# Layer 0's down projections at sixteen pairs of row and weight places with three wider products each; output tiles innermost and stepped sums elsewhere

## The chip, the core and the metric

The kernel runs on one core of one Trainium2 chip. TensorE (PE) multiplies, VectorE (DVE) and ScalarE (ACT) prepare operands and take sums out of PSUM, GpSimd (POOL) does small copies, SyncE (SP) issues the transfers of the weights. The metric is the device time of one execution in microseconds; three runs of the kernel before gave 2278.22, 2278.60 and 2279.71.

## What is computed

A decoder of two layers over 272 positions (16 meta tokens and 256 inputs) with model width 2048, 16 heads of 128 and an MLP of width 8192. Layer 0 is a forgetting attention, layer 1 a stick-breaking attention over shared keys and values.

```python
for layer in range(2):
    a = rms_norm(h, norm_attn[layer])
    ...                       # attention of the layer, its output projection added to h
    h = h + squared_relu_mlp(rms_norm(h, norm_mlp[layer]), w_up[layer], w_down[layer])
return rms_norm(h, final_norm)[:, N_META:]

def squared_relu_mlp(h, w_up, w_down):
    u = h @ w_up
    return jnp.square(jax.nn.relu(u)) @ w_down
```

Everything is in float32. Only the 256 inputs are returned, so the kernel drops the 16 meta positions from layer 1's queries on.

## The kernel before

Activations lie feature-major: 16 chunks of 128 features on the partitions, positions along the free axis. Every projection is a run of `gemm_group` calls (line 174). One call makes 512 output features, four tiles `acc` of 128 features, from all 16 chunks of the input and one block of weights. To keep float32 accuracy with the single-pass type fp32r, rows and weights are each split in a high and a low part, and a product is three matmuls: weight high by row high, weight high by row low, weight low by row high. So a call issues 4 tiles x 16 chunks x 3 = 192 matmuls, each with a weight load of its own, and the 96 calls issue 18,432, all recorded at line 162 in the helper `gemm_matmul`. That helper also chains each matmul behind the one before it, so TensorE's order is the order in which the code writes them (except in the first call, where the scheduler orders them).

A call goes through its 16 chunks in four blocks `kb` of four. In blocks 0 and 3 all chunks of one output tile come before the next tile. In blocks 1 and 2 the weights come in two halves of two chunks; within a half the code before runs for `m` (output tile), for `kc` (chunk), for the three pairs of parts. Layer 1's calls (`t0` = 16) run the pairs of parts outermost. Weights arrive by SP's queue in `raw`, ACT writes the high part `whi` (line 214), DVE the low part `wlo` (line 215), each as 128 x 1024 elements; four buffers of each.

Two lengths of product occur. Calls for all positions (`t0` = 0: layer 0, the shared keys and values) stream 272 columns, calls for layer 1's inputs (`t0` = 16) stream 256.

Where operands lie is written out by hand. The class `Split` (line 99) holds the high and low rows of one activation, 640 numbers a chunk; `ROWS` says where in the chunk they begin: high at 48 and low at 368 for 272 columns, 0 and 320 for 256 columns. Weights begin at number 0 of their tile for 272 columns and at number 16 for 256. All tiles and strides are multiples of 64 numbers (256 bytes), so counted modulo 64 the rows begin 48 after the weights in both cases.

For 256 columns there is one thing more. In every second call the argument `widen` makes three of the first block's products six columns longer (262; line 234, `over`). The six columns beyond the row are zeros that POOL copied there (line 114, `SPAN` = 6), and the sums in them are not used. Calls of 272 columns have no such products.

The MLP (`mlp`) runs four slices `f` of 2048 hidden features; each slice is four up calls (from `xm`, writing the new `Split` `u`) and four down calls (from `u`, adding to `hT`).

Of the kernel before, what the change touches and what calls it, by code (L numbers as in the profile page):

```python
# [9 lines left out]
F32 = mybir.dt.float32  # L10
# [5 lines left out]
P = 128  # L16
D = 2048
NC = D // P
M = 16
# [8 lines left out]
SPAN = 6  # L28
# [6 lines left out]
def yoco_kernel(ctx: ExitStack, tc: tile.TileContext, hT_in, gains, b_f, w_f, w_qkv0, w_o0, w_up, w_dn,  # L35
# [63 lines left out]
    class Split:  # L99


        def __init__(self, label, t0):
            n = T - t0
            self.t0 = t0
            rows = xs.tile([P, NC * XROW + 64], F32R, tag="x", name=f"x_{label}")
            hi, lo = ROWS[t0]
            o = min(hi, lo)
            rows = rows[:, o:o + NC * XROW].rearrange("p (c t) -> p c t", c=NC)
            self.hi, self.lo = (rows[:, :, k - o:k - o + n] for k in (hi, lo))

            if t0:
                self.wide = {}
                for name, k in (("hi", hi), ("lo", lo)):
                    nc.gpsimd.tensor_copy(rows[:, 0, k - o + n:k - o + n + SPAN], pad[:, :SPAN])
                    self.wide[name] = rows[:, 0, k - o:k - o + n + SPAN]

    def split_chunk(sp, gi, c):

# [51 lines left out]
        tc.add_manual_dep(ins.ins, queued[0].name, mybir.DependencyInfo(mybir.DependencyClass.NoSync,  # L170
                                                                        mybir.DependencyReason.DATA))

    def gemm_group(wblk, sp, t0, evac, before={}, after={}, load_x=None, widen=False):

        uid[0] += 1
        u = uid[0]  # L180
        accs = [pacc.tile([P, 512], F32, tag="acc", name=f"acc_{u}_{m}") for m in range(4)]
        n = T - t0
        for kb in range(4):
            src_w = wblk[kb].rearrange("p (k c) -> p k c", k=4)
            if kb in before:
                before[kb]()
            piece = 1 if load_x is not None and kb < 2 else 2
            raws = [wraw.tile([P, 2, 512], F32, tag="raw", name=f"raw_{u}_{kb}_{hf}") for hf in range(2)]
            for k0 in range(0, 4, piece):
                if load_x is not None:  # L190
                    load_x(range(4 * kb + k0, 4 * kb + k0 + piece))
                if load_x is not None and kb == k0 == 0:

                    for c0 in (0, 256):
                        nc.scalar.dma_start(raws[0][:, 0, c0:c0 + 256], src_w[:, 0, c0:c0 + 256])
                else:
                    nc.sync.dma_start(raws[k0 // 2][:, k0 % 2:k0 % 2 + piece], src_w[:, k0:k0 + piece])
            parts = []
            for hf in range(2):
                whi = wspl.tile([P, 2 * 576], F32R, tag="whi", name=f"whi_{u}_{kb}_{hf}")  # L200
                wlo = wspl.tile([P, 2, 576], F32R, tag="wlo", name=f"wlo_{u}_{kb}_{hf}")
                if t0:
                    whi = whi.rearrange("p (k c) -> p k c", k=2)[:, :, 16:528]
                    wlo = wlo[:, :, 16:528]
                else:
                    whi = whi[:, :1024].rearrange("p (k c) -> p k c", k=2)
                    wlo = wlo[:, :, :512]
                boxes = [(o, piece, 0, 512) for o in range(0, 2, piece)]
                if load_x is not None and kb == hf == 0:
                    boxes[:1] = [(0, 1, 0, 256), (0, 1, 256, 512)]  # L210
                for o, no, c0, c1 in boxes:
                    src = raws[hf][:, o:o + no, c0:c1]
                    hp, lp = whi[:, o:o + no, c0:c1], wlo[:, o:o + no, c0:c1]
                    on_act = nc.scalar.activation(hp, src, AF.Copy)  # L214
                    on_dve = nc.vector.tensor_tensor(out=lp, in0=src, in1=hp.bitcast(F32), op=ALU.subtract)  # L215
                parts.append((whi, wlo))
            if kb in after:
                with tc.issue_after(on_act.ins), tc.issue_after(on_dve.ins):
                    after[kb]()


            if load_x is not None and kb == 0:
                runs = [([kc], range(4)) for kc in range(4)]
            elif kb in (0, 3):
                runs = [(range(4), [m]) for m in range(4)]
            else:
                runs = [(range(2 * hf, 2 * hf + 2), range(4)) for hf in range(2)]
            pinned[0] = load_x is None
            for kcs, ms in runs:
                if t0:  # L230
                    series = [(w, x, kc, m) for w, x in ((0, "hi"), (0, "lo"), (1, "hi")) for m in ms for kc in kcs]
                else:
                    series = [(w, x, kc, m) for m in ms for kc in kcs for w, x in ((0, "hi"), (0, "lo"), (1, "hi"))]
                for i, (w, x, kc, m) in enumerate(series):
                    over = SPAN if widen and kb == m == 0 and i in (0, 4, 8) else 0
                    rhs = sp.wide[x] if over else getattr(sp, x)[:, 4 * kb + kc]
                    gemm_matmul(accs[m][:, :n + over], parts[kc // 2][w][:, kc % 2, m * P:(m + 1) * P], rhs,
                                start=kb == kc == w == 0 and x == "hi", stop=kb == kc == 3 and w == 1)
                if kb == 3:
                    for m in ms:  # L240
                        evac(m, accs[m][:, :n])
# [297 lines left out]
    def mlp(layer, xm, norm, t0, last_evac):  # L539
# [3 lines left out]
            box["r"] = norm.finish()  # L543

        for f in range(N_FF):
            u = Split(f"u{layer}_{f}", t0)
            for g in range(4):
                def evac(m, acc, g=g):
                    c = 4 * g + m
                    r = tmp.tile([P, T], F32, tag="relu", name=f"relu_{layer}_{f}_{c}")  # L550
                    u2 = tmp.tile([P, T], F32, tag="u2", name=f"u2_{layer}_{f}_{c}")
                    nc.vector.scalar_tensor_tensor(out=r[:, t0:], in0=acc, scalar=0.0, in1=box["r"][:, t0:],
                                                   op0=ALU.max, op1=ALU.mult)
                    nc.scalar.activation(u2[:, t0:], r[:, t0:], AF.Square)
                    nc.scalar.activation(u.hi[:, c], u2[:, t0:], AF.Copy)
                    nc.vector.tensor_tensor(out=u.lo[:, c], in0=u2[:, t0:], in1=u.hi[:, c].bitcast(F32),
                                            op=ALU.subtract)
                gemm_group(w_up[layer, f, g], xm, t0, evac, {2: get_rstd} if f == g == 0 else {},
                           widen=t0 == M and g % 2 == 1)
            for g in range(4):  # L560
                def evac(m, acc, g=g):
                    residual_add(4 * g + m, acc, t0)
                    if f == N_FF - 1:
                        last_evac(4 * g + m)
                gemm_group(w_dn[layer, f, g], u, t0, evac, widen=t0 == M and g % 2 == 1)

    xm, norm_m = out_proj(w_o0, ao, 0, G_M0, "m0", late, turning)

# [182 lines left out]
```

## Time and profile before

| | |
|---|---|
| median of three runs | 2278.60 us |
| the profiled execution | 2278.99 us |
| its span, first to last instruction | 2277.3 us |
| mean granted TensorE clock | 0.998 |
| TensorE busy in the span | 2265.0 us |
| VectorE, ScalarE busy | 1360.6 us, 1111.8 us |
| layer 0's MLP, 32 calls | 418.4 to 1176.6 us from the span's start |
| of it the first slice's four down calls | 513.6 to 608.3 us |
| shared keys and values, 8 calls | 1264.7 to 1473.9 us |

A matmul's record reads about 280 ns because its end is modelled with the pipeline's depth, and records overlap. What a matmul costs is the distance from its start to the next start. It is read by dividing a window by the number of matmuls in it, or from two rows of the timeline (start, length, count): the difference of the starts by the count of the first row.

### The profile page before, as it was taken

The page shows a single profiled execution, that of the slowest core. Times are in us where ns is not written, and L with a number is a line of the kernel's source. Part 1 is how long each engine was busy: PE and PEld are TensorE (multiplying, and loading weights), DVE is VectorE, ACT ScalarE, POOL GpSimd, SP SyncE. Part 2 cuts the span into 40 slices and gives each one's busy share as a digit, 9 for nine tenths or more (in the row PEclk, how much of TensorE's full clock was granted, in tenths as well). Part 3 has the DMA queues.
Part 4 walks back from the last instruction along what each step waited for, and adds up shares of the span by engine and source line. Part 5 has one row for each costly group of instructions (what it writes and reads, how often), then busy time and mean ns, then how long its engine had stood idle before and what let it go on. Part 6 is the DMA issues. An engine that isn't in the chain of part 4 may idle for free.

```text
span 2277.3 us, 44746 instructions
## 1 busy us (share of the span) xinstructions
PE 2265.0 (99%) x18882; PEld 2259.6 (99%) x18882; DVE 1360.6 (60%) x1909; ACT 1111.8 (49%) x1533; POOL 32.8 (1%) x75
## 2 busy tenths in 40 slices
PE   9999999999999999999999999999999999999998
PEld 9999999999999999999999999999999999999998
DVE  7777676555454455455566677766555555555554
ACT  6654554443354344344444567655544443544553
POOL 1000000000000000000000000000000000000000
PEclk9999999999999999999999999999999999999999
DMA  7555555555555555555565544455656656556563
GB/s 237 178 163 168 182 167 161 182 180 171 185 172 186 179 169 186 175 185 178 170 192 181 180 160 156 160 189 184 198 187 195 200 190 201 189 188 203 184 203 130
DMA packets 116905, 412.32 MB, mean 181 GB/s; under 512 B 13520, under 2 KB 16992, under 8 KB 116704
## 3 DMA queue, kind: packets, MB, share of 16 engines
q1 hardware_dynamic: 114560, 406.29, 55.3%
q10 hardware_dynamic: 2144, 3.17, 0.5%
q8 instruction: 148, 2.42, 0.4%
q14 instruction: 53, 0.43, 0.1%
HBM read 407.29 MB, written 2.11 MB: 180 GB/s over the span
## 4 chain that ended last, share of the span: by engine, by line
PE 99%; DMA 1%; DVE 0%; ACT 0%; issue 0%; DVEq 0%; SPq 0%; ACTq 0%
PE acc L162 96%; PE po L406 1%; PE ps L338 1%; DMA raw<-w_qkv 1%; PE ps L336 0%; PE po L409 0%; DMA hT<-hT_in 0%; PE po L410 0%; DVE ob L693 0%; PE pf L285 0%; PE pf L286 0%; ACT whi L214 0%; PE pms_fin L650 0%; DVE ob L690 0%; ACT x_o L430 0%; PE pms_a L143 0%
## 5 line engine op out<-in xcount | busy, mean ns | idle before, releaser
L215 DVE TENSOR_TENSOR wlo<-raw,whi 128x1024 fp32r<-128x1024 f32 (+1 forms) x773 | 927.4, 1216 | 674.1 <-ACT whi L214 666.9
L214 ACT ACTIVATE whi<-raw 128x1024 fp32r<-128x1024 f32 (+1 forms) x773 | 797.3, 1051 | 942.5 <-PE acc L162 909.5
L162 PE MATMUL acc<-x_m,whi 128*128 128x272 f32 (+1 forms) x4096 | 643.2, 281 | 0.0
L162 PE MATMUL acc<-x_u,whi 128*128 128x272 f32 (+1 forms) x4096 | 642.9, 281 | 0.0
L162 PEld LDWEIGHTS acc<-x_m,whi 128*128 128x128 f32 x4096 | 566.0, 188 | 0.1
L162 PEld LDWEIGHTS acc<-x_u,whi 128*128 128x128 f32 x4096 | 565.8, 188 | 0.0
L162 PE MATMUL acc<-x_m,wlo 128*128 128x272 f32 (+1 forms) x2048 | 440.9, 281 | 0.0
L162 PE MATMUL acc<-x_u,wlo 128*128 128x272 f32 (+1 forms) x2048 | 440.8, 281 | 0.0
L162 PE MATMUL acc<-x_a,whi 128*128 128x272 f32 (+1 forms) x2048 | 353.6, 286 | 0.5 <-ACT whi L214 0.4
L162 PEld LDWEIGHTS acc<-x_m,wlo 128*128 128x128 f32 x2048 | 323.4, 188 | 0.0
L162 PEld LDWEIGHTS acc<-x_u,wlo 128*128 128x128 f32 x2048 | 323.3, 188 | 0.0
L162 PEld LDWEIGHTS acc<-x_a,whi 128*128 128x128 f32 x2048 | 300.5, 188 | 1.5 <-ACT whi L214 1.3
L162 PE MATMUL acc<-x_a,wlo 128*128 128x272 f32 (+1 forms) x1024 | 253.1, 285 | 0.0
L162 PE MATMUL acc<-x_kv,whi 128*128 128x272 f32 x1024 | 192.6, 287 | 0.0
L162 PEld LDWEIGHTS acc<-x_a,wlo 128*128 128x128 f32 x1024 | 175.6, 188 | 0.7 <-issue 0.5
L162 PE MATMUL acc<-x_o,whi 128*128 128x272 f32 (+1 forms) x1024 | 162.6, 283 | 0.7 <-ACT x_o L430 0.4
L162 PEld LDWEIGHTS acc<-x_kv,whi 128*128 128x128 f32 x1024 | 160.0, 188 | 0.0
L162 PE MATMUL acc<-x_kv,wlo 128*128 128x272 f32 x512 | 147.1, 287 | 0.0
L162 PEld LDWEIGHTS acc<-x_o,whi 128*128 128x128 f32 x1024 | 142.0, 188 | 1.4 <-DVE x_o L431 0.7
L244 DVE TENSOR_TENSOR hT<-acc,hT 128x272 f32<-128x272 f32 (+1 forms) x160 | 69.1, 432 | 86.3 <-PE acc L162 86.2
L162 PE MATMUL acc<-x_o,wlo 128*128 128x272 f32 (+1 forms) x512 | 110.5, 282 | 0.0
L162 PEld LDWEIGHTS acc<-x_kv,wlo 128*128 128x128 f32 x512 | 96.5, 188 | 0.0
(180 smaller groups left out, 1062.0 us busy)
## 6 DMA issues: line engine op xcount, KB each, us to landing
raw<-w_up SPq DMA_DIRECT2D x256, 512.0 KB, 4.6
raw<-w_dn SPq DMA_DIRECT2D x256, 512.0 KB, 4.6
raw<-w_qkv SPq DMA_DIRECT2D x92, 512.0 KB, 3.8
raw<-w_o SPq DMA_DIRECT2D x64, 512.0 KB, 4.3
raw<-w_kv SPq DMA_DIRECT2D x64, 512.0 KB, 4.5
raw<-w_q SPq DMA_DIRECT2D x32, 512.0 KB, 4.7
fk<-f_dram ACTq DMA_DIRECT2D x4, 544.0 KB, 5.9
raw<-w_qkv SPq DMA_DIRECT2D x7, 256.0 KB, 4.9
```

The lines of the kernel that those rows point to most:

```text
L162: ins = nc.tensor.matmul(*args, **kw).ins
L214: on_act = nc.scalar.activation(hp, src, AF.Copy)
L215: on_dve = nc.vector.tensor_tensor(out=lp, in0=src, in1=hp.bitcast(F32), op=ALU.subtract)
L244: nc.vector.tensor_tensor(out=hT[:, c, t0:], in0=acc, in1=hT[:, c, t0:], op=ALU.add)
L338: nc.tensor.matmul(ps[:, 144:416], qs[a][:, j, :], ks[b][:, j, :], start=i == 0, stop=i == 2)
L406: ins = nc.tensor.matmul(po[:, i, :], v[:, j, 0, :], p[:, j, :2 * P], start=i == 0, stop=False)
```

## The change

Three things change, all in `Split`, `gemm_group` and the calls from `mlp`.

1. A new argument `place`. In layer 0's MLP the rows of slice `f` begin at 16f (low part at 16f + 320) in place of 48 and 368, and the weights of down call `g` begin at 16g in place of 0. So the sixteen down calls of layer 0 have the sixteen pairs (16f, 16g). Their weights are written as two runs of 512 with a stride of 576, the form that layer 1 has.
2. In those sixteen calls, in block 2, three matmuls of 278 columns are added ahead of the products number 0, 7 and 14 of the first half. Each writes a tile `push` of its own that nothing reads, from the weights of the product it precedes and from chunk 8's row with six more columns of zeros; POOL writes those zeros when the `Split` is made.
3. In all other calls of 272 columns, blocks 1 and 2 run for `kc`, for the three pairs of parts, for `m`: the output tile is innermost. And except in the very first call the sums of tile `m` begin at column `step * m` of their PSUM tile, with `step` 16, 48, 32 or 0 by the call's number.

```diff
-        def __init__(self, label, t0):
+        def __init__(self, label, t0, place=None):
...
-            hi, lo = ROWS[t0]
+            hi, lo = ROWS[t0] if place is None else (place, place + 320)
...
-            if t0:
+            if t0 or place is not None:
                 self.wide = {}
+                c = 0 if t0 else 8
                 for name, k in (("hi", hi), ("lo", lo)):
-                    nc.gpsimd.tensor_copy(rows[:, 0, k - o + n:k - o + n + SPAN], pad[:, :SPAN])
-                    self.wide[name] = rows[:, 0, k - o:k - o + n + SPAN]
+                    nc.gpsimd.tensor_copy(rows[:, c, k - o + n:k - o + n + SPAN], pad[:, :SPAN])
+                    self.wide[name] = rows[:, c, k - o:k - o + n + SPAN]
...
-    def gemm_group(wblk, sp, t0, evac, before={}, after={}, load_x=None, widen=False):
+    def gemm_group(wblk, sp, t0, evac, before={}, after={}, load_x=None, widen=False, place=None):
...
         n = T - t0
+        step = 0 if t0 or load_x is not None or place is not None else (0, 16, 48, 32)[u % 4]
+        accs = [a[:, step * m:] for m, a in enumerate(accs)]
...
+                elif place is not None:
+                    whi = whi.rearrange("p (k c) -> p k c", k=2)[:, :, place:place + 512]
+                    wlo = wlo[:, :, place:place + 512]
...
+                elif len(kcs) == 2 and place is None:
+                    series = [(w, x, kc, m) for kc in kcs for w, x in ((0, "hi"), (0, "lo"), (1, "hi")) for m in ms]
                 else:
                     series = [(w, x, kc, m) for m in ms for kc in kcs for w, x in ((0, "hi"), (0, "lo"), (1, "hi"))]
                 for i, (w, x, kc, m) in enumerate(series):
                     over = SPAN if widen and kb == m == 0 and i in (0, 4, 8) else 0
+                    if place is not None and kb == 2 and kcs[0] == 0 and i in (0, 7, 14):
+                        push = patt.tile([P, 512], F32, tag="patt", name=f"push_{u}_{i}")
+                        gemm_matmul(push[:, :n + SPAN], parts[0][w][:, 0, m * P:(m + 1) * P], sp.wide[x],
+                                    start=True, stop=True)
...
-            u = Split(f"u{layer}_{f}", t0)
+            u = Split(f"u{layer}_{f}", t0, None if layer else 16 * f)
...
-                gemm_group(w_dn[layer, f, g], u, t0, evac, widen=t0 == M and g % 2 == 1)
+                gemm_group(w_dn[layer, f, g], u, t0, evac, widen=t0 == M and g % 2 == 1, place=None if layer else 16 * g)
```

How TensorE's order changes is seen at two places. The first is the first down call of layer 0 (call 21), first half of block 2. Names are output <- row, weights; `acc_21_0` is the sum of output tile 0, `x_u0_0` the rows of slice 0. Before:

```order
L162 MATMUL acc_21_0_6131<-x_u0_0_5045,whi_21_2_0_6259 128x272 x2
L162 MATMUL acc_21_0_6131<-x_u0_0_5045,wlo_21_2_0_6260 128x272
L162 MATMUL acc_21_0_6131<-x_u0_0_5045,whi_21_2_0_6259 128x272 x2
L162 MATMUL acc_21_0_6131<-x_u0_0_5045,wlo_21_2_0_6260 128x272
L162 MATMUL acc_21_1_6132<-x_u0_0_5045,whi_21_2_0_6259 128x272 x2
L162 MATMUL acc_21_1_6132<-x_u0_0_5045,wlo_21_2_0_6260 128x272
```

And now:

```order
L163 MATMUL push_21_0_6269<-x_u0_0_5045,whi_21_2_0_6261 128x278
L163 MATMUL acc_21_0_6133<-x_u0_0_5045,whi_21_2_0_6261 128x272 x2
L163 MATMUL acc_21_0_6133<-x_u0_0_5045,wlo_21_2_0_6262 128x272
L163 MATMUL acc_21_0_6133<-x_u0_0_5045,whi_21_2_0_6261 128x272 x2
L163 MATMUL acc_21_0_6133<-x_u0_0_5045,wlo_21_2_0_6262 128x272
L163 MATMUL acc_21_1_6134<-x_u0_0_5045,whi_21_2_0_6261 128x272
L163 MATMUL push_21_7_6278<-x_u0_0_5045,whi_21_2_0_6261 128x278
L163 MATMUL acc_21_1_6134<-x_u0_0_5045,whi_21_2_0_6261 128x272
L163 MATMUL acc_21_1_6134<-x_u0_0_5045,wlo_21_2_0_6262 128x272
```

The products stand in the same order as before, with three wider ones put between them (the third follows after seven more products).

The second is an up call of layer 0 (call 18), first half of block 1; `x_m0` is the MLP's input. Before:

```order
L162 MATMUL acc_18_0_5327<-x_m0_3919,whi_18_1_0_5395 128x272 x2
L162 MATMUL acc_18_0_5327<-x_m0_3919,wlo_18_1_0_5396 128x272
L162 MATMUL acc_18_0_5327<-x_m0_3919,whi_18_1_0_5395 128x272 x2
L162 MATMUL acc_18_0_5327<-x_m0_3919,wlo_18_1_0_5396 128x272
L162 MATMUL acc_18_1_5328<-x_m0_3919,whi_18_1_0_5395 128x272 x2
L162 MATMUL acc_18_1_5328<-x_m0_3919,wlo_18_1_0_5396 128x272
```

And now:

```order
L163 MATMUL acc_18_0_5329<-x_m0_3919,whi_18_1_0_5397 128x272
L163 MATMUL acc_18_1_5330<-x_m0_3919,whi_18_1_0_5397 128x272
L163 MATMUL acc_18_2_5331<-x_m0_3919,whi_18_1_0_5397 128x272
L163 MATMUL acc_18_3_5332<-x_m0_3919,whi_18_1_0_5397 128x272
L163 MATMUL acc_18_0_5329<-x_m0_3919,whi_18_1_0_5397 128x272
L163 MATMUL acc_18_1_5330<-x_m0_3919,whi_18_1_0_5397 128x272
L163 MATMUL acc_18_2_5331<-x_m0_3919,whi_18_1_0_5397 128x272
L163 MATMUL acc_18_3_5332<-x_m0_3919,whi_18_1_0_5397 128x272
```

The same 24 products of the half now go round the four sums, one row part four times in a row, where before six products in a row went to one sum. SP's queue stands as before; POOL has eight small copies more, two for each of the four `u` tiles.

## The prediction

> **What bounds the kernel now.** I read the page first: busy time, the clock by slices, the chain that ended last. "..." stands for lines left out.
>
> ```profile
> span 2277.3 us, 44746 instructions
> PE 2265.0 (99%) x18882; PEld 2259.6 (99%) x18882; DVE 1360.6 (60%) x1909; ACT 1111.8 (49%) x1533; POOL 32.8 (1%) x75
> ...
> PEclk9999999999999999999999999999999999999999
> ...
> PE acc L162 96%; PE po L406 1%; PE ps L338 1%; DMA raw<-w_qkv 1%; PE ps L336 0%; PE po L409 0%; DMA hT<-hT_in 0%; PE po L410 0%; DVE ob L693 0%; PE pf L285 0%; PE pf L286 0%; ACT whi L214 0%; PE pms_fin L650 0%; DVE ob L690 0%; ACT x_o L430 0%; PE pms_a L143 0%
> ```
>
> TensorE is without work for 2277.3 - 2265.0 = 12.3 us, its clock is full in every slice, and 96% of the chain are the projections' matmuls. So the time is the number of matmuls times the distance between their starts. The second view is therefore that distance by stage, from windows of the matmuls that write `acc` (from:to, length, busy and count for each engine).
>
> ```profile
> core 0: us, PE busy (x) PEld busy (x) DVE busy (x) ACT busy (x), PEclk, DMA share, GB/s
> 418.40:1176.60 758.20, 758.11 (x6146) 757.87 (x6145) 56.30 (x128) 0.00 (x0) 1.00 0.55 178
> 513.60:608.30 94.70, 94.70 (x771) 94.70 (x770) 7.04 (x16) 0.00 (x0) 1.00 0.54 179
> 1191.00:1199.00 8.00, 8.00 (x70) 8.00 (x69) 1.27 (x3) 0.00 (x0) 1.00 0.61 196
> 1264.70:1473.90 209.20, 196.38 (x1538) 191.86 (x1537) 13.75 (x32) 0.00 (x0) 1.00 0.49 161
> 1676.00:2176.00 500.00, 500.00 (x4412) 500.00 (x4412) 38.99 (x92) 0.00 (x0) 1.00 0.61 194
> ```
>
> Four down calls hold 4 x 192 = 768 products (the row counts a few that reach in from outside): 94.70 / 768 = 123.3 ns for 272 columns. Layer 0's whole MLP has 6144 in 758.2 us, 123.4 ns. Layer 1, with 256 columns, takes 500 / 4412 = 113.3 ns. But in the third row, also 256 columns, it is 8.00 / 68 = 117.6 ns (two of the 70 reach in). The third view shows when that ends: the timeline of TensorE at 1199 us, where the first three widened products stand (start, length, count).
>
> ```profile
> 1197.85 1.10 PE L162 MATMUL acc<-x_a,whi 128*128 128x256 f32 x8
> 1198.79 0.63 PE L162 MATMUL acc<-x_a,wlo 128*128 128x256 f32 x4
> 1199.26 1.12 PE L162 MATMUL acc<-x_a,whi 128*128 128x262 f32 x8
> 1200.21 0.64 PE L162 MATMUL acc<-x_a,wlo 128*128 128x262 f32 x4
> 1200.69 1.07 PE L162 MATMUL acc<-x_a,whi 128*128 128x256 f32 x8
> 1201.60 0.62 PE L162 MATMUL acc<-x_a,wlo 128*128 128x256 f32 x4
> ...
> 1242.87 1.08 PE L162 MATMUL acc<-x_a,whi 128*128 128x262 f32 x8
> 1243.79 0.62 PE L162 MATMUL acc<-x_a,wlo 128*128 128x262 f32 x4
> 1244.25 1.07 PE L162 MATMUL acc<-x_a,whi 128*128 128x256 f32 x8
> ```
>
> Ahead of them twelve products take 1199.26 - 1197.85 = 1.41 us, 117.5 each; behind them eight take 1201.60 - 1200.69 = 0.91 us, 113.8. So the same products on the same places have two rates, which last, and three products with six columns more bring TensorE from the slower to the faster. That is what the change tries at 272 columns, at sixteen places.
>
> **The change part by part.** The sixteen down calls stay 16 x 192 = 3072 products. Added are 16 x 3 = 48 of 278 columns, on the engine that is never idle, so each costs its whole distance. No row has 278 columns. The nearest is a product of 272 at 123.3 ns. What six columns add is in the last three rows above: twelve products, three of them widened, take 1244.25 - 1242.87 = 1.38 us against 12 x 113.3 = 1.36, so 20 ns for three, some 7 ns each. The ends are 123.3 (six columns free) and 130; I take 128, nearer to the row that shows widened products. 48 x 128 ns = **6.1 us**; ends 5.9 and 6.2.
>
> Around a wide product the settled rhythm is broken for a few products. In the rows above that is inside the 20 ns already counted; I add nothing.
>
> The places themselves are the unknown term. Before, all products of 272 columns have rows 48 after weights (modulo 64), whatever tile they use. Of the sixteen pairs (16f, 16g) four keep that difference, those with f - g = 3 or -1; twelve calls, 12 x 192 = 2304 products, have differences of 0, 16 or 32 that no row shows. The nearest price is the step between the two rates at 256 columns, 117.6 - 113.3 = 4.3 ns. If all twelve calls lay one such step higher, 2304 x 4.3 = 9.9 us more; one such step lower, 9.9 us less. Nothing in the trace says which: 123.3 stands between nothing known below and nothing known above. So I take **0** and keep both ends.
>
> The Trainium skill ("TensorE: Matmul & The Clock Gate", Step-by-step: what each phase is for) says that TensorE has two independent read ports, and that loading the next tile's weights takes no read bandwidth from the running matmul. By that rule places cannot matter, the term is exactly 0 and the pushes are all. The two rates at 256 columns, 117.6 and 113.3, stand at equal places, so they neither bear it out nor refute it, but they show something that the rule does not have.
>
> The weights of these calls are now written in two runs of 512. The same form stands in layer 1 already: ACT takes 1059 there and 1056 ns in layer 0.
>
> ```profile
> L214 ACT ACTIVATE whi<-raw 128x1024 fp32r<-128x1024 f32 x34 | 35.1, 1056 | 60.4 <-PE acc L162 60.4
> ...
> L214 ACT ACTIVATE whi<-raw 128x1024 fp32r<-128x1024 f32 x37 | 38.3, 1059 | 49.7 <-PE acc L162 49.7
> ```
>
> These are windows of 100 us in layer 0's and layer 1's MLP. Most of ACT's idle time ends when TensorE frees a buffer, so 8 pieces a call, 8 x 1.06 = 8.5 us of a call's 23.7, stay under the products: 0.
>
> POOL gets eight copies more, like those it makes for layer 1:
>
> ```profile
> L114 POOL CAST x_u<-pad 128x6 fp32r<-128x6 f32 x8 | 1.3, 191 | 613.5 <-PE acc L162 613.5
> ```
>
> They wait for the last reader of the buffer, as this row does. Behind them on POOL stand only the copies for the next slices and for layer 1's attention, and the first push that needs them comes four up calls later, 4 x 23.7 = 95 us. Cost 0; without that cover it would be 2 x 0.19 us a slice.
>
> The new order in blocks 1 and 2 concerns the other 40 calls of 272 columns. What it costs is shown by the first of them, whose order the scheduler made before and which goes round the four output tiles already. Its second block on the timeline:
>
> ```profile
> 12.04 1.26 PE L162 MATMUL acc<-x_a,whi 128*128 128x272 f32 x8
> 13.14 0.66 PE L162 MATMUL acc<-x_a,wlo 128*128 128x272 f32 x4
> 13.63 1.15 PE L162 MATMUL acc<-x_a,whi 128*128 128x272 f32 x8
> 14.62 0.66 PE L162 MATMUL acc<-x_a,wlo 128*128 128x272 f32 x4
> 15.11 1.15 PE L162 MATMUL acc<-x_a,whi 128*128 128x272 f32 x8
> ```
>
> From 13.63 to 15.11 twelve products take 1.48 us: 123.3 ns, no more and no less than elsewhere. So the order is worth 0. That the sums begin at columns 16 to 144 of their tiles has no row; since neither one sum twelve times in a row nor four sums in turn moves the rate, I take 0 too. Its ends are wide, one step of 4.3 ns on the 29 calls that have a `step` over 0, 29 x 192 = 5568 products, 24 us either way, and I give them a small chance.
>
> In the attention calls the scheduler sets some of the score products a few places later among the projections' products. They are the same products, and all the waiting of TensorE in the whole span is 12.3 us; I take 0, with 1 us either way.
>
> **The sum.** 2278.99 (the profiled execution; its span and 1.7 us around it) + 6.1 = 2285.1. The median of the runs shown is 0.4 lower, so I forecast **2284.7 us**, +0.27%.
>
> **The rivals.** First, *other places are slower*. For it: 123.3 is 10 ns over the 113.3 of 256 columns though 16 columns more would be 16/256 of that, 7 ns; so the distance holds waiting that depends on something. Against it: no row shows another place. One step on the twelve calls gives 2284.7 + 9.9 = 2294.6; on half of them 2289.7.
>
> Second, the other side: *the wide products do at 272 columns what they do at 256*. The mechanism sits in block 2 of each down call: after the third push the remaining products run a step of 4.3 ns faster. About 80 products remain in a call; 16 x 80 x 4.3 = 5.5 us, which nearly pays the pushes: 2279.2. It decides from the point where the state outlives the call. At 256 columns it does, the fast rate of the row at 1676 us goes on through call after call. Then the up calls between (12 x 192) and the first halves of the later down calls (15 x 110) gain as well, 3954 x 4.3 = 17.0 us: 2262. For it: the rows at 1199 us. Against it stands a window in the shared keys and values, 95 us after layer 0 and behind a stage of 256 columns and the queries' norm:
>
> ```profile
> 1270.00:1288.00 18.00, 18.00 (x148) 18.00 (x148) 1.32 (x3) 0.00 (x0) 1.00 0.62 198
> ```
>
> 18.00 us / 146 (two reach in) is again 123.3 ns: whatever breaks the rhythm between, 272 columns come back to the same rate, and a second one shows nowhere. Also the places change from call to call, which may undo the state.
>
> The skill's page named above (Back-to-back issue gap) gives N/2.4 + 2.5 ns, an estimate of 115.8 ns for 272 columns and 109.2 for 256; the rows have 123.3 and 113.3, so by that page there is even more to win than one step: 3072 x 7.5 = 23 us if the sixteen calls reached it.
>
> Third, *the stepped sums change the rate* of the other calls, with its ends of 24 us; half a step slower would be 2296.7.
>
> **How the numbers follow.** A difference under 0.2%, 4.6 us, cannot be told from no change in this kernel. Slower than that begins at 2283.2, faster at 2274.0. Chances: the forecast, pushes alone with places that about cancel, 0.55 (2281 to 2288); slower places 0.20 (2288 to 2296); pushes that pay for themselves within the calls 0.13 (2276 to 2283); a faster state that lasts 0.07 (below 2274); stepped sums 0.05, of which slower 0.03. Slower by over 0.2%: 0.50 of the forecast's 0.55, and 0.20 and 0.03 beside it: 0.73. Within 0.2%: 0.05 + 0.12 = 0.17. Faster: 0.07, a little of the third case and of stepped sums, 0.10. The range of 8 in 10 runs from the pushes just paid for to most of the slower places: 2278 to 2294.
>
> **What would show it.** In the profile after, the sixteen down calls should take 23.68 us each plus 0.38 for three pushes, 94.7 + 1.5 = 96.2 us a slice. A call that takes more shows a pair of places with a slower rate, one with less a faster. Calls of equal difference f - g should agree if only the difference matters. The halves before and behind the pushes of one call should have the same rate if the pushes change nothing; if the second half is faster and the next up call too, the second rival is right. The up calls and the shared keys and values should keep 123.3 ns; if they do not, the order or the stepped sums count after all and my reading of the first call was wrong. The prediction fails if a slice is off 96.2 by more than 1 us on average.

## The result and the profile after

The changed kernel takes 2291.32 us (four runs, 2291.07 to 2293.65) against 2278.41 before (four runs). The ratio is 1.0058 with a 95% interval of 1.0046 to 1.0071: 12.9 us slower. The forecast was 2284.7 in a range of 2278 to 2294, so direction and range held, and the forecast had half of the increase.

The page of the changed kernel, the lines that answer to those shown of before:

```profile
span 2289.3 us, 44853 instructions
PE 2276.9 (99%) x18930; PEld 2272.0 (99%) x18930; DVE 1358.4 (59%) x1909; ACT 1111.6 (49%) x1533; POOL 32.2 (1%) x83
...
PEclk9999999999999999999999999999999999999999
```

TensorE has 48 matmuls more and is still the engine without a pause: 2289.3 - 2276.9 = 12.4 us without work against 12.3, at full clock. So the 12 us more in the span are distances between starts of products. Where they lie, windows of the matmuls that write `acc` show (from:to, length, then busy and count of each engine, TensorE first; further down TensorE alone; the last three numbers are clock, DMA share and GB/s). First the four down slices, each the four calls of a row place, the first, the last and the sum:

```profile
512.90:610.80 97.90, 97.90 (x771) 97.14 (x769) 7.04 (x16) 0.00 (x0) 1.00 0.53 172
...
1090.80:1188.80 98.00, 98.00 (x771) 97.25 (x770) 7.04 (x16) 0.00 (x0) 1.00 0.53 172
sum 391.80, PE 391.80 PEld 388.79 DVE 28.15 ACT 0.00; mean PE 97.95 PEld 97.20 DVE 7.04 ACT 0.00
```

391.8 us, where four slices of 94.7 make 378.8: the sixteen calls have grown by 13.0 us, and no other stage has grown. The span grew by 12 and not 13 because the attention stage ahead ended 0.7 us earlier; the rest lies in the tenths of the windows. The up calls between two slices, layer 0's new order in them, take what they took, the shared keys and values 209.3 us against 209.2, layer 1 is the same (these three rows count all instructions):

```profile
610.80:705.50 94.70, 94.70 (x770) 94.70 (x769) 49.91 (x62) 44.21 (x62) 0.31 (x2) 1.00 0.55 178
1276.80:1486.10 209.30, 209.30 (x1684) 208.68 (x1683) 160.66 (x236) 138.18 (x188) 3.18 (x16) 1.00 0.50 161
1676.00:2176.00 500.00, 500.00 (x4412) 500.00 (x4411) 273.23 (x320) 223.60 (x272) 0.94 (x6) 1.00 0.61 194
```

Now call by call, the first slice (0, 0), (0, 1), (0, 2), (0, 3) and the third, (2, 0) to (2, 3); windows from a call's first product to the next call's first.

```profile
512.90:537.30 24.40, 24.40 (x194) 1.00 0.53 173
537.30:561.40 24.10, 24.10 (x194) 1.00 0.55 175
561.40:586.10 24.70, 24.70 (x195) 1.00 0.51 171
586.10:610.80 24.70, 24.70 (x195) 1.00 0.53 171
...
898.20:922.90 24.70, 24.70 (x195) 1.00 0.54 171
922.90:947.60 24.70, 24.70 (x195) 1.00 0.53 170
947.60:972.00 24.40, 24.40 (x194) 1.00 0.53 173
972.00:996.10 24.10, 24.10 (x194) 1.00 0.56 175
```

Each call had 23.7 before. The pattern is that of the difference between row place and weight place. Counted modulo 64 it is 0, 48, 32, 16 in the first slice and 32, 16, 0, 48 in the third: 24.1 us at 48, 24.4 at 0, 24.7 at 16 and 32, whatever the places themselves are. All sixteen calls follow it. The 24.1 at difference 48 is the old rate with the pushes; the others have a rate of their own besides.

The pushes change none of these rates. Call (0, 2), difference 32, on the timeline (start, length, count; two rows ahead of its three pushes and two behind them):

```profile
569.00 0.42 PE L163 MATMUL acc<-x_u,whi 128*128 128x272 f32 x2
...
572.04 0.42 PE L163 MATMUL acc<-x_u,whi 128*128 128x272 f32 x2
...
576.60 0.42 PE L163 MATMUL acc<-x_u,whi 128*128 128x272 f32 x2
...
579.64 0.42 PE L163 MATMUL acc<-x_u,whi 128*128 128x272 f32 x2
```

Between the rows of each pair lie 24 products: 3.04 us or 126.7 ns, ahead of the pushes and behind them.

### The profile page after: what moved, and what is told of

Its sections match the earlier page's. It is cut to its first block, busy times and chain, and to the rows that moved or that the text cites. A ratio compares the mean times of both kernels' runs of the same rounds, so it can differ in the third digit from the quotient of the medians.

```text
span 2289.3 us, 44853 instructions
## 1 busy us (share of the span) xinstructions
PE 2276.9 (99%) x18930; PEld 2272.0 (99%) x18930; DVE 1358.4 (59%) x1909; ACT 1111.6 (49%) x1533; POOL 32.2 (1%) x83
## 4 chain that ended last, share of the span: by engine, by line
PE 99%; DVE 0%; DMA 0%; ACT 0%; SPq 0%; issue 0%; DVEq 0%; ACTq 0%
PE acc L163 96%; PE po L418 1%; PE ps L350 1%; PE ps L348 0%; PE po L421 0%; PE push L163 0%; DMA raw<-w_qkv 0%; PE po L422 0%; DVE ob L705 0%; PE pf L297 0%; PE pf L298 0%; PE pms_fin L662 0%; DVE ob L702 0%; ACT x_o L442 0%; PE pms_a L144 0%; PE pms_m L144 0%
## 5 line engine op out<-in xcount | busy, mean ns | idle before, releaser
L163 PE MATMUL acc<-x_m,whi 128*128 128x272 f32 (+1 forms) x4096 | 601.2, 282 | 0.0
L163 PEld LDWEIGHTS acc<-x_m,whi 128*128 128x128 f32 x4096 | 541.7, 188 | 0.1
L163 PE MATMUL acc<-x_m,wlo 128*128 128x272 f32 (+1 forms) x2048 | 378.5, 282 | 0.0
L163 PE MATMUL acc<-x_a,whi 128*128 128x272 f32 (+1 forms) x2048 | 322.6, 285 | 0.7 <-ACT whi L220 0.7
L163 PEld LDWEIGHTS acc<-x_m,wlo 128*128 128x128 f32 x2048 | 298.7, 188 | 0.0
L163 PEld LDWEIGHTS acc<-x_a,whi 128*128 128x128 f32 x2048 | 282.6, 188 | 1.8 <-ACT whi L220 0.9
L163 PE MATMUL acc<-x_a,wlo 128*128 128x272 f32 (+1 forms) x1024 | 209.3, 285 | 0.0
L163 PE MATMUL acc<-x_kv,whi 128*128 128x272 f32 x1024 | 171.7, 288 | 0.0
L163 PE MATMUL acc<-x_kv,wlo 128*128 128x272 f32 x512 | 115.8, 287 | 0.0
L564 DVE SCALAR_TENSOR_TENSOR relu<-acc,rstd_m 128x272 f32<-128x272 f32 (+1 forms) x128 | 55.3, 432 | 69.1 <-PE acc L163 69.0
```

Of the source, the lines that this page charges most:

```text
L163: ins = nc.tensor.matmul(*args, **kw).ins
```

## The experiments

**Places alone.** The kernel before with the new places and nothing else of the change.

```diff
...
-            hi, lo = ROWS[t0]
+            hi, lo = ROWS[t0] if place is None else (place, place + 320)
...
-                gemm_group(w_dn[layer, f, g], u, t0, evac, widen=t0 == M and g % 2 == 1)
+                gemm_group(w_dn[layer, f, g], u, t0, evac, widen=t0 == M and g % 2 == 1, place=None if layer else 16 * g)
```

> The sixteen pairs of places alone, on the kernel before: no wide products, old order, sums at column 0. Theory A (the rate of a call hangs on the difference of row place and weight place modulo 64 and on nothing else): calls with difference 48 take 23.68 us, with 0 24.06, with 16 and 32 24.32; the sixteen together 4 x 23.68 + 4 x 24.06 + 8 x 24.32 = 385.5 against 378.9 before, so the whole +6.6 us, about 2285.1. Rival B (the wide products leave TensorE in a slower state that lasts until the places change back): without them all sixteen calls take 23.68 and the time is that of before.

2286.03 us against 2278.44, ratio 1.0031 (1.0020 to 1.0043). The calls (0, 0), (0, 1), (0, 2), then (1, 2), and the first call of layer 1:

```profile
513.20:537.30 24.10, 24.10 (x194) 1.00 0.53 175
537.30:561.60 24.30, 24.30 (x194) 1.00 0.52 173
561.60:585.90 24.30, 24.30 (x194) 1.00 0.53 174
753.40:777.10 23.70, 23.70 (x195) 1.00 0.53 178
...
1183.60:1206.70 23.10, 23.01 (x195) 1.00 0.55 183
```

Theory A holds for fifteen calls and rival B falls: no wide product, and the slower rates are there. But two rows are not in A. Call (0, 1) has difference 48 and should take 23.7; it took 24.3. And the queries' first call, which nothing in this kernel changes, took 23.1 where it had 22.7. So a call can also be caught in a rate that is not that of its places; what catches it these rows do not show. The two make 1.0 us of the 7.6. The seven runs fall in two groups, three at 2285.2 to 2285.3 and four, the profiled one among them, at 2286.0 to 2286.3; this would fit runs without and with the caught calls, but no run of the first group was profiled.

**Pushes alone.** The kernel before with the three products of 278 columns, places 48 and 0.

```diff
...
+                    if pushes and kb == 2 and kcs[0] == 0 and i in (0, 7, 14):
+                        push = patt.tile([P, 512], F32, tag="patt", name=f"push_{u}_{i}")
+                        gemm_matmul(push[:, :n + SPAN], parts[0][w][:, 0, m * P:(m + 1) * P], sp.wide[x],
+                                    start=True, stop=True)
...
```

> The three wide products in each of layer 0's down calls alone, on the kernel before: places 48 and 0, old order, sums at column 0. Theory A: each call 24.07 us, the sixteen +6.2 us, about 2284.6, and 123.3 ns a product ahead of and behind the pushes. Rival B: calls after the first push run at 125 to 127 ns, each call 24.4 to 24.7, +12 to +16 us.

2285.46 us, ratio 1.0030 (1.0019 to 1.0042). The first and the last of the four slices in windows (the two between have 96.3 as well):

```profile
513.90:610.20 96.30, 96.30 (x770) 1.00 0.53 175
...
1087.00:1183.40 96.40, 96.40 (x771) 1.00 0.53 175
```

Each slice is 1.6 us longer, 133 ns for each of twelve pushes, and all four are alike, 6.4 us together; B, which wanted each slice to grow by 3 to 4 us, is out. Pushes and places add up to the change: 6.4 us here, and 13.0 - 6.4 = 6.6 for places, which is, within the tenths of these windows, what the four calls at 0 and the eight at 16 and 32 take above 23.7 without pushes, 4 x 0.4 + 8 x 0.6 = 6.4.

**The third part alone.** Order and stepped sums in the other calls.

```diff
...
+        step = 0 if t0 or load_x is not None or place is not None else (0, 16, 48, 32)[u % 4]
+        accs = [a[:, step * m:] for m, a in enumerate(accs)]
...
+                elif len(kcs) == 2 and place is None:
+                    series = [(w, x, kc, m) for kc in kcs for w, x in ((0, "hi"), (0, "lo"), (1, "hi")) for m in ms]
...
```

> The third part of the change alone: output tile innermost in blocks 1 and 2 and sums at stepped columns in all calls of 272 columns but layer 0's down calls; old places, no added products. Theory A: 23.68 us a call in layer 0, the time that of before within 1 us. Rival J (the order wins something in the attention stage, whose end came 0.7 us earlier in the changed kernel): 0.5 to 1 us faster in every run.

2279.15 us, ratio 1.0002 (0.9993 to 1.0012): nothing. Layer 0's MLP has 6144 matmuls in a window of 758.0 us, 123.4 ns. The 0.7 us by which the attention stage ended earlier in the changed kernel are no gain of the order: the first down call begins anywhere from 512.7 to 513.9 us in kernels that have the old order there, and at 512.9 in this one and in the changed kernel.

**Places in steps of 4, twice.** Rows at 48, 52, 56, 60 by weights at 0, 4, 8, 12 in layer 0, first without, then with three wide products in block 1 of each call. The first run, whose diff this is, also moved layer 1's places.

```diff
...
-            u = Split(f"u{layer}_{f}", t0)
+            u = Split(f"u{layer}_{f}", t0, 4 * f + (0 if layer else 48))
...
+                gemm_group(w_dn[layer, f, g], u, t0, evac, widen=t0 == M and g % 2 == 1, place=4 * g + (16 if layer else 0))
```

> The kernel before, where only places of the down projections change, in steps of 4 numbers: in layer 0 (272 columns) rows at 48, 52, 56, 60 for the four slices by weights at 0, 4, 8, 12 for the four calls; in layer 1 (256 columns) rows at 0, 4, 8, 12 by weights at 16, 20, 24, 28. Theory A as far as the whole of the difference counts: the four calls of a diagonal agree with (48, 0) and (0, 16), that is 23.68 and 21.76 to 21.78 us, and the others lie between these and the next steps of 16 (24.06 to 24.32 for 272 columns). Rival C (a start that is no multiple of 16 costs in itself, since a row of 272 or 256 numbers then takes one more stretch of 16): even on the diagonal (52, 4) is slower, by up to 16 of 296 parts, 1.3 us a call. A call under 23.68 would be a better place than that of before. Whole time 2276 to 2300.

> The map of layer 0 in steps of 4 numbers once more, rows at 48, 52, 56, 60 by weights at 0, 4, 8, 12, now with three wide products in block 1 of each call; layer 1 as before. Theory A with K (the difference alone sets the rate, and 126.7 on the diagonal was a state that a call was caught in): behind the wide products (52, 4), (56, 8) and (60, 12) go to 123.3 ns. Rival C (a start off the multiples of 16 costs in itself): (52, 4) and (60, 12) stay at 126.7. No place under 123.3 by either.

Without wide products, the diagonal (48, 0), (52, 4), (56, 8), (60, 12):

```profile
512.90:536.60 23.70, 23.70 (x194) 1.00 0.53 178
728.00:752.30 24.30, 24.30 (x194) 1.00 0.53 174
943.40:967.10 23.70, 23.70 (x195) 1.00 0.54 178
1158.50:1182.80 24.30, 24.30 (x194) 1.00 0.53 173
```

By itself this would be rival C, though (56, 8) is no multiple of 16 either. With wide products the timeline of (52, 4) decides it (start, length, count; the first two rows stand ahead of the pushes, the last two begin 46 products behind the third of them):

```profile
732.16 0.42 PE L163 MATMUL acc<-x_u,whi 128*128 128x272 f32 x2
...
735.20 0.42 PE L163 MATMUL acc<-x_u,whi 128*128 128x272 f32 x2
...
736.35 0.29 PE L163 MATMUL push<-x_u,whi 128*128 128x278 f32 x1
...
744.15 0.41 PE L163 MATMUL acc<-x_u,whi 128*128 128x272 f32 x2
...
747.11 0.41 PE L163 MATMUL acc<-x_u,whi 128*128 128x272 f32 x2
```

Between each pair of rows lie 24 products: 3.04 us or 126.7 ns ahead of the pushes, 2.96 us or 123.3 ns behind them. Call (60, 12) does the same. So 272 columns have two lasting rates at difference 48, and here wide products ended the slower one. On the diagonal A holds in steps of 4, and C falls. Off the diagonal the rates were 123.3 to 126.7, some other in the second run than in the first ((52, 8) had 23.7 us without wide products, and stayed at 126.7 behind them), so a rate off the diagonal says little about its places. Nor do wide products always lead to the faster rate: (56, 0) had 125.4 ns ahead of them and 126.7 behind. In layer 1, which the first run also moved, the diagonal had 113.3 ns in three calls and 117.8 in (8, 24), which has no widened products; the others had 116.7 to 120.0. The two kernels took 2299.29 and 2290.83 us, one run each. No call of layer 0 in either run is under 23.7 us, none of layer 1 under the 21.76 of before: no place tried is better than that of before.

**Freeing a caught call.** The places alone, with wide products in call (0, 1) only, block 1.

```diff
...
+                gemm_group(w_dn[layer, f, g], u, t0, evac, widen=t0 == M and g % 2 == 1, place=None if layer else 16 * g, pushes=layer == f == 0 and g == 1)
```

> As the run with the sixteen pairs of places alone, in which call (0, 1) of layer 0's down projections, difference 48, ran at 126.7 ns from first to last and took 24.32 us; now three wide products stand in that one call, in the first half of its block 1. Theory K (272 columns too have two lasting rates at difference 48, 123.3 and 126.7, and wide products can end the slower): block 0 at 126.7, blocks 2 and 3 at 123.3, the call 23.68 + 0.40 + some 0.2 us. Rival L (126.7 belongs to that pair of places under this layout): 126.7 behind the wide products too, 24.7 us.

It could not answer: this time call (0, 1) ran at 123.3 from its first product on and took 23.7 and the pushes, though TensorE's instructions ahead of it were the same (2286.69 us in one run). So TensorE's instructions alone do not fix whether a call is caught; what does is open, since the two kernels also differ in POOL's copies. The second run in steps of 4 above answered instead.

**Other pushes, and the sixteen pairs in layer 1.** In layer 0 one or three narrower products a call, 270 to 256 columns; in layer 1 the pairs (16f, 16g).

```diff
...
+                        short = n - 2 * (kick % 8 + 1)
+                        gemm_matmul(push[:, :short], parts[0][w][:, 0, m * P:(m + 1) * P],
+                                    getattr(sp, x)[:, 8, :short], start=True, stop=True)
...
```

> The kernel before with narrower added products in layer 0's down calls at the places 48 and 0: calls 0 to 7 have one product of 270, 268, ... 256 columns, calls 8 to 15 three of the same widths. In layer 1 the down calls get the sixteen pairs (16f, 16g), with the widened products of before in every second call. Theory A: no added product changes the rate at 272 columns, calls take 23.80 with one and 24.04 with three; in layer 1 the calls of difference 48 keep 21.76 to 21.78 and the others are slower, by 0.4 to 0.9 us. Rival D (272 columns have a faster state that only another kick reaches): behind one of the widths the rate falls from 123.3 to about 120 ns, and the next up calls keep it.

2298.15 us in one run. Layer 0: 23.8 us with one, 24.0 to 24.1 with three, 123.3 ns ahead and behind at every width; rival D falls for these widths. Layer 1, the calls (0, 0) to (0, 3) in the first four rows, (1, 0) to (1, 2) in the others; their differences are 0, 48, 32, 16 and 16, 0, 48:

```profile
1657.60:1680.70 23.10, 23.10 (x195) 1.00 0.57 182
1680.70:1702.50 21.80, 21.80 (x195) 1.00 0.60 194
1702.50:1725.30 22.80, 22.80 (x195) 1.00 0.58 186
1725.30:1747.90 22.60, 22.60 (x194) 1.00 0.58 187
1835.00:1856.70 21.70, 21.70 (x194) 1.00 0.60 193
1856.70:1879.70 23.00, 23.00 (x194) 1.00 0.59 186
1879.70:1902.40 22.70, 22.70 (x195) 1.00 0.57 186
```

At 256 columns difference 0 is the worst (23.0 to 23.1), 32 next (22.8); 48 has 21.8 or 22.7, and 16 has 22.6 or 21.7. I had expected 48 to hold 21.8 and the others to lie above; 16 does not, and 48 has the faster rate only in the two of its four calls that have widened products. At difference 16 the two calls with widened products stayed at 22.6, so there these did not end the slower rate. The ranking is another than at 272 columns.

**No widened products in layer 1.**

```diff
...
-                           widen=t0 == M and g % 2 == 1)
+                           widen=False)
...
```

> The kernel before without the widened products in layer 1. Theory A with two states at 256 columns: after the queries' norm the calls stay at 117.8 ns, 22.62 us a call, through layer 1: 47 of the 48 calls of 256 columns at most, 41 of them by 0.85 us, +35 us, some 2313. Rival I (TensorE finds the faster state by itself soon): at most a few calls at 117.8, under +4 us.

2306.54 us in one run, +28 us: once disturbed by a norm, calls stay at 117.8 ns, from the MLP's norm on to the end of layer 1. The same 500 us that held 4412 products before hold

```profile
1676.00:2176.00 500.00, 500.00 (x4248) 1.00 0.58 187
```

Rival I falls. The estimate of 35 was too high because layer 1's output projection is not among the slow calls: its last three calls ran at 113.3 ns with no widened product, behind the attention's last products. So 34 whole calls were at 117.8, 29 us.

**Low parts moved apart.** High rows and weights stay; low rows 16f further, low weights 16g.

```diff
...
-            hi, lo = ROWS[t0]
+            hi, lo = ROWS[t0][0], ROWS[t0][1] + shift
...
+                    wlo = wlo[:, :, o + shift:o + shift + 512]
...
```

> The kernel before; in the down projections the high rows and high weights keep their places and the low rows lie 16f further, the low weights 16g further. Two theories on which places meet. Theory E (a product's rows meet the weights that are loaded under it, those of the next product): the row of products goes weight high by row high, weight high by row low, weight low by row high; under the first and the third the next load is of high weights, under high rows, which keep their difference; under the second it is of low weights under low rows. So the four calls with f = g keep 23.68 us in layer 0, and of the others a third of the products are off, by 2.0 to 3.4 ns: 23.8 to 23.9. Theory F (a product's rows meet its own weights): low rows by high weights and high rows by low weights matter; only f = g = 0 keeps 23.68, calls with f = 0 or g = 0 have a third of the products off, all others two thirds, 24.0 to 24.1.

2295.92 us in one run. Calls (0, 0), (0, 1) and (1, 1):

```profile
513.20:536.90 23.70, 23.70 (x194) 1.00 0.55 178
536.90:561.20 24.30, 24.30 (x194) 1.00 0.53 174
...
727.80:751.90 24.10, 24.10 (x194) 1.00 0.55 176
```

E is refuted: (1, 1), where low meets low at the old difference, is 0.4 us slower, and (2, 2) and (3, 3) are 0.2 and 0.3 slower. F has the one unharmed call right and not the sizes: (0, 1) has 24.3 and (3, 2) too, (2, 1) 23.9. Some of these may be caught calls, which one run cannot tell. Adding up thirds of the products explains the sixteen calls in neither form; that a rate belongs to the rhythm of the whole sequence is a guess that would fit.

**Half the weight load.** The sixteen pairs, 64 of 128 weight columns a load.

```diff
...
-                    gemm_matmul(accs[m][:, :n + over], parts[kc // 2][w][:, kc % 2, m * P:(m + 1) * P], rhs,
+                    gemm_matmul(accs[m][:cols, :n + over], parts[kc // 2][w][:, kc % 2, m * P:m * P + cols], rhs,
...
```

> The sixteen pairs of places alone, and each weight load of layer 0's down projections takes 64 of the 128 columns, so half of these outputs is left out. Theory M (rows being streamed meet the weights being loaded, and the waiting of one for the other makes the rate): with half as long a load the places differ by less than half of the 3.4 ns between 123.3 and 126.7, and all rates come down, towards 120. Rival N (places act through the stream alone, whatever is loaded): 123.3, 125.3 and 126.7 as before.

2281.21 us in one run; half of these outputs is left out. Calls (0, 0) to (0, 2):

```profile
512.90:536.70 23.80, 23.80 (x194) 1.00 0.56 177
536.70:560.60 23.90, 23.90 (x194) 1.00 0.55 177
560.60:584.50 23.90, 23.90 (x194) 1.00 0.52 176
```

All sixteen calls lie at 23.8 to 23.9, 124.0 to 124.5 ns. The spread of places falls from 3.4 ns to 0.5: N falls. But M said the rates would come down towards 120, and those of difference 48 went up, from 123.3 to 124.0 in one call and 124.5 in three; the four calls of difference 0 are now among the best, at 124.0. That rows wait for weights in some simple way is not shown. Half the load also means half the rows of sums written, and no run takes these two apart.

**Longer products.** The down calls stream 0 to 30 columns of zeros more.

```diff
...
+                    if longer is not None:
+                        over = longer
+                        rhs = sp.longer[x][:, 4 * kb + kc, :n + over]
...
```

> The kernel before; the down projections stream more columns than they need, zeros behind the row, 0, 2, 4 ... 30 more by the call, so 272 to 302 in layer 0 and 256 to 286 in layer 1; places as before, and layer 1's down calls without the three widened products of before. Theory G (what a product takes above its columns hangs on the length, since rows and weights must come back into step): the distance does not grow by 0.83 ns for two columns but in flats and steps, and some length over 272 takes no more than 123.3 ns or less. Rival H (a fixed share on top of the columns): 0.83 ns more for every two columns, 135.8 at 302.

2337.93 us in one run. Calls of 272, 274, 284, 286 and 296 columns:

```profile
512.70:536.40 23.70, 23.70 (x194) 1.00 0.55 179
536.40:560.70 24.30, 24.30 (x194) 1.00 0.54 173
...
754.00:779.60 25.60, 25.60 (x194) 1.00 0.51 165
779.60:803.90 24.30, 24.30 (x194) 1.00 0.52 174
1096.40:1123.30 26.90, 26.90 (x195) 1.00 0.48 157
```

The distance goes in steps and even falls: 284 columns take 25.6 us a call, 286 take 24.3, as much as 274. H, a fixed share on top, is out; of G the steps hold, but no longer product takes 123.3 or less. The steps are no caught calls: layer 1's down calls reach the same lengths and have the same distances within 0.5 ns for 272 to 286 columns (123.3 at 272, 126.7 at 274, 133.3 at 284 and 126.7 again at 286). At 256 columns the step is greater: 113.3, and 120.8 with two columns more.

**All weights and rows 128 bytes further, no widened products.** In the run with longer products the disturbed calls of layer 1 went back to 113.3 ns by themselves. That kernel had a small tile of zeros ahead of weights and rows, which shifts all of them by 128 bytes.

```diff
+    gap = align.tile([P, 32], F32, name="gap")
+    nc.gpsimd.memset(gap, 0.0)
...
-                           widen=t0 == M and g % 2 == 1)
+                           widen=False)
...
```

> The kernel before without any widened product, and with 32 numbers more in the pool that stands ahead of weights and rows, so that all of them lie 128 bytes further; their differences stay. In the run with longer products, which had this shift by accident, the calls that are disturbed by a norm or by attention went back to 113.3 ns by themselves. Theory O (which of the two rates follows a disturbance depends on how the addresses of the disturbing products and of these calls stand to each other): layer 1 at 113.3 throughout, 1.5 us less in the three disturbed calls and those behind them and 0.5 us less for widened products: 2276.5, 0.1% faster than before. Rival P (it was the longer products that did it): 117.8 from the queries' norm on as in the run without widened products, 2306.

The profiled execution has a span of 2276.1 us and, once each disturbance is over, the faster rate throughout layer 1 with no widened product:

```profile
1200.00:1264.00 64.00, 64.00 (x567) 1.00 0.62 198
1676.00:2176.00 500.00, 500.00 (x4415) 1.00 0.61 194
```

But over eleven runs it is no better than before: median 2277.67 against 2278.32, ratio 1.0001 (0.9992 to 1.0010). Seven runs lie at 2276.8 to 2277.8, four at 2280.5 to 2281.6. A stretch of four or five calls at 117.8, 0.85 us each, would make these 4 us, but none of those four was profiled. P falls, since all eleven runs lie far under the 2306.54 of the same kernel without the shift. Of O it is shown that the shift matters; how the addresses act is not. As measured this kernel does not beat the kernel before, and none tried does.

## Why the prediction was right, and where it was off

- *What bounds the kernel*: right. All of the change shows as distance between TensorE's products; idle time stayed at 12.4 us.
- *The pushes, 48 x 128 ns = 6.1 us*: right in kind, a little small in size. Alone they cost 6.4 us in the windows, just over the upper end of 6.2: 133 ns each, so 10 ns more than a product of 272 and not the 5 that were taken.
- *"Nothing in the trace says which ... So I take 0"*: this is the term that was mis-sized. It measured 6.6 us. The first rival priced one step of 4.3 ns on all twelve calls of another difference, 9.9 us; the step is 3.4 ns at differences 16 and 32 and 2.0 at 0, eight and four calls. 48, where the kernel already stood, is the best of the four. The trace of before, with 272 columns at this one difference alone, could not tell the sign.
- *The Trainium skill's rule of two independent ports* ("TensorE: Matmul & The Clock Gate", Step-by-step: what each phase is for) would have made the term exactly 0. Here the measurement decides: with the same products, rates of 123.3, 125.3 and 126.7 ns follow the difference of row and weight place. The Trainium skill's N/2.4 + 2.5 ns (same page, Back-to-back issue gap), an estimate of 115.8 for 272 columns, is reached at no place tried. The page gives that formula for an isolated matmul and not for a stream of weight loads and matmuls, which this kernel is, so it was no measure of what could be won.
- *The second rival, wide products do at 272 columns what they do at 256*: its mechanism exists, as (52, 4) shows, and it was wrong to conclude from one window that 272 columns come back to the same rate whatever breaks the rhythm. But the second rate at difference 48 is the slower one, 126.7. The kernel before was not caught in it, so its pushes had nothing to end; and the calls of other differences kept their rates behind the pushes. That is why it earned nothing.
- *Order, stepped sums, weights in two runs, POOL's copies, score products: 0 each*: right for the first two by a run of their own (1.0002), for the others by the windows, in which no other stage grew and calls of difference 48 keep 123.3 ns with weights in two runs.
- *"Calls of equal difference should agree"*: they do in the changed kernel, all sixteen; with the places alone one did not.
- *"The prediction fails if a slice is off 96.2 by more than 1 us on average"*: by this sign of its own it failed. The slices took 97.9 to 98.0, 1.7 us more, for the places.

The forecast's first case, "pushes alone with places that about cancel", had a chance of 0.55 and was half the truth; the time came out in the second case's band, 2288 to 2296, which had 0.20. Half of the increase, and with it the direction, was forecast for the right reason. That the range held is owed to the slower places being counted in its upper part, not to the sum.

## What to carry to other kernels

Where TensorE never waits, look at the distance from one matmul's start to the next: 123.3 or 126.7 ns shows in no busy share, and such differences made 0.3% here, as much as the added products. When a stage of equal matmuls shows two rates that last, it is worth varying where the two operands begin against each other, which moved the rate here while the output's order and place did not; compare whole calls by their starts. A probe that puts many variants in one run is cheap, but its calls can inherit a rate from what ran ahead of them, so each variant needs a second look from another starting point.

## What the runs showed of the hardware that was not expected

- At 272 columns of fp32r with a load of 128 columns each, the distance is 123.3, 125.3, 126.7, 126.7 ns for rows 48, 0, 16, 32 numbers behind weights modulo 64; at 256 columns 113.3 or 117.8 at 48 and 16, 118.7 at 32, 120.0 at 0. In steps of 16 with high and low parts moved alike, only the difference counted: moving both by the same 16 left these rates as they are, and moving everything by 128 bytes left the 123.3 and the 113.3. In steps of 4, or with low parts moved against high, calls had other rates besides.
- The rate has a memory. 256 columns stayed at 117.8 for 31 calls in a row where nothing pushed them (4248 products in 500 us against 4412), and 272 columns stayed at 126.7 for a whole call at places that also run at 123.3. Which rate follows a disturbance changed when all weights and rows were moved by 128 bytes.
- Two columns more cost 3.4 ns from 272 to 274 and 7.5 from 256 to 258, and saved 6.7 from 284 to 286 (25.6 to 24.3 us a call).
- What gets into step is open. The runs show that the difference of the operands' starts and the length of the stream take part in it, that halving the load together with the rows of sums leaves 0.5 of the 3.4 ns between places, and that the output tile's order and place change nothing (1.0002).
